# FFN output product in another order, one weight sum gathered early in loose slots, half-width rest rows, and sums of input weights begun elsewhere

## The chip, the cores and the metric

The kernel runs on one core of a Trainium2 chip. The metric is the device time of one execution in microseconds (us); a smaller number is better.

## What is computed

Two layers of a streaming encoder with 512 positions and 1024 channels. Each layer has a token mixer (three attention-like branches) and then an FFN. The change lies in the FFN alone:

```
u = einsum('bsd,df->bsf', x, w_ffn_in[l])          # 1024 -> 2 x 2816
u_gate, u_up = split(u, 2)
ffn = einsum('bsf,fd->bsd', silu(u_gate) * u_up, w_ffn_out[l])   # 2816 -> 1024
x = layer_norm(DEEPNORM_ALPHA * x + ffn, ln2_g[l], ln2_b[l])
```

## The kernel before

**Arithmetic.** Everything is float32. A matmul operand is split into a high and a low part in float32r, and a product is three matmuls (`mm3`, L125 to L127: high by high, and the two mixed ones). The high part is a cast on ScalarE (`wh`, L315 for a whole block, L157 for a Wt block), the low part a subtraction on VectorE (`wl`, L322, L158).

**Products by a two-by-two scheme.** A large product is cut into two by two blocks and made from seven products of sums of blocks in place of eight, in Winograd's form. The seven are called m1, m2, y, x, v, g and h. Each needs one weight block of 128 x 2048 elements (1 MB), which is a block of the weights or a sum of them, and each is 24 matmuls of 512 columns. Four of them add on to a bank that an earlier one left: x, then g, then h on m1's, and v on y's. VectorE reads such a bank between two of them (L1301 adds it to a row of the residual `z`; L852 and L857 do the same for the FFN's input). So v may not begin before VectorE has read y's banks.

**Where the sums come from.** A block is loaded by a DMA from the SP queue (`load`, L177) into a staging slot `st`, of which there are four. A second block is added to it in place by an accumulating DMA from the GpSimd queue (`more`, L181). In the class Chain, which FFN-out uses, one buffer serves m1, y, x and h in turn: when m1's block has been split, the next weights are accumulated onto it for y, then for x, then for h, so each of the accumulations waits for the split before it, and the next split for the accumulation. Its block c (for g) is a load and an accumulation in a staging slot of its own. In the class Close, which FFN-in uses, there are also a (for y) and c (for g), each a load and an accumulation.

**Order.** A list at the end of `layer` names the items in the order in which TensorE takes them. Each product is an item, with groups of small steps that are issued between its halves; `["c"]` and `["a"]` among them start a load and an accumulation. Blocks are split up to three items ahead (AHEAD = 3 buffers of `wh` and `wl`). Every engine and every queue works strictly in its own order: an instruction that waits holds all behind it.

**Names.** p, q, r and u are the four FFN-in groups (512 columns each, gate and up); t is the fifth one, whose 512 columns are not twinned into two-by-two products on the way out (its hidden blocks 16 to 19; blocks 20 and 21 come from `u_ffn`). o and w are the two FFN-out groups, of 8 hidden blocks each; `u_rest(0)` and `u_rest(1)` are the product of hidden blocks 16 to 21 with the remaining rows of w_ffn_out, for the left and the right half of the columns. Each u_rest has a block of four row tiles and a block of two. I write "w.y" for product y of group w, and so on. `s_hid` splits hidden blocks 16 to 21 for u_rest. `s_turn` transposes gate times up back with TensorE, in the middle of a product. Single tiles of 128 x 512 (activations, residual rows) come from another pool, `g`, with 61 slots.

Around the change the order before was: ... p.g, t.v, p.h, t.x, q.m1, t.g, q.y, t.h, q.v, q.m2, q.x, r.m1, q.g, r.y ..., and at the end of the layer ... u_rest(0), o.v, o.x, w.m1, o.g, w.m2, o.h, w.y, w.v, w.x, u_rest(1), w.g, w.h.

Of the kernel before, what the change touches and what calls it, by code (L numbers as in the profile page):

```python
# [17 lines left out]
P = 128  # L18
# [40 lines left out]
def trunk(ctx, tc, x_in, xT_in, w_in, ret_norm_g, da_norm_g, lq1, lk1, lq2, lk2, w_a, w_b, w_c, b_merge, w_out,  # L59
# [20 lines left out]
    def g(dt=F32, name="g"):  # L80
        return gp.tile([P, 512], dt, tag="g", name=name)
# [42 lines left out]
    def mm3(ps, lh, ll, rh, rl, start, stop, onto=False):  # L124
        nc.tensor.matmul(ps, lh, rh, start=start, stop=False, skip_group_check=onto)  # L125
        nc.tensor.matmul(ps, lh, rl, start=False, stop=False, skip_group_check=onto)  # L126
        nc.tensor.matmul(ps, ll, rh, start=False, stop=stop, skip_group_check=onto)  # L127
# [32 lines left out]
    class Halves:  # L160
# [30 lines left out]
        def g(self):  # L191
            return self.block(self.__dict__.pop("c"))

    class Chain(Halves):


# [34 lines left out]

        def h(self):
            return self.block(self.__dict__.pop("a"))

    class Close(Halves):

# [456 lines left out]
    def layer(l):  # L693
# [742 lines left out]
        def s_turn(pb, hf):  # L1436

            def fn():
                rows = [nat.pop((pb, 2 * hf + j)) for j in range(2)]
                for fp in range(2):  # L1440
                    ps = bank("ph")
                    for i in range(2):
                        for j in range(2):
                            o, c = 256 * i + P * j, P * (2 * fp + i)
                            nc.tensor.transpose(ps[:, o:o + P], rows[j][:, c:c + P], ident)
                    t = half[pb, hf, fp] = g(name="hf")
                    nc.scalar.copy(t, ps)
            return fn
# [11 lines left out]
        def s_differ(gi, fp):  # L1460
            def fn():
                twins[gi, fp].difference(half.pop((2 * gi + 1, 1, fp)))
            return fn

        def s_sums(gi, fp):
            def fn():
                twins[gi, fp].sums()
            return fn
# [6 lines left out]
        def s_hid(*ids):  # L1475
            def fn():
                for i in ids:
                    t, hid[i] = hid[i], Pair("hid")
                    split(hid[i], t)
            return fn  # L1480
# [13 lines left out]
        def s_natural(*ts):  # L1494
            def fn():
                for t in ts:
                    x1["n"].natural(t)
            return fn
# [20 lines left out]
        def fout_items(gi):  # L1519

            r0, kh = GROUPS[gi]
            hv = Chain(w_ffn_out[l], r0, kh)
            w = {}

            def it(name, *adds):
                def fn(wt):
                    if name == "m1" and gi == 0:
                        load_res(x2, saved[2 * l])
                        x2["n"] = Norm(x2["z"], v["g2"], v["b2"], None, None, xTs[l + 1],
                                       out if last else saved[2 * l + 1], xfs[l + 1])  # L1530
                    on = {"x": "m1", "g": "m1", "h": "m1", "v": "y"}.get(name, name)
                    final = gi == len(GROUPS) - 1 and name in ("m2", "g", "h")
                    for j in range(2):
                        end = last and final and name != "m2" and j
                        ps = w.pop((on, j), None)
                        for cols in (A, B) if end and name == "h" else (slice(0, 512),):
                            ps = product([hid[r0 + k] for k in range(kh)], name, j, wt, ps, cols)
                            for i, hf, op in adds:
                                plus(x2, 2 * i + j, hf, ps[:, cols], op, final, cols,
                                     (A, B) if end and name == "g" else (cols,))  # L1540
                        if name not in ("m2", "v", "h"):
                            w[on, j] = ps
                        if final and name == "h":
                            closed(2 + j)
                        between()
                    if final and name == "h" and not last:
                        quarters(l + 1)
                        ahead[nc.vector] = last_of(nc.vector)
                        behind[opening_fn[l + 1]] = list(ahead.values())
                return [getattr(hv, name)], fn  # L1550

            add, sub = ALU.add, ALU.subtract
            return {"c": hv.ahead_c, "m1": it("m1", (0, 0, add)), "y": it("y", (1, 1, add)), "x": it("x", (0, 1, sub)),
                    "m2": it("m2", (0, 0, add)), "v": it("v", (0, 1, add)), "g": it("g", (1, 1, sub)), "h": it("h", (1, 0, add))}

        ahead = {}
# [10 lines left out]
        def u_rest(hf):  # L1567

            rk = FT - REST - 4
            c0 = 512 * hf  # L1570
            blocks = [([w_ffn_out[l][P * REST:P * REST + P * 4, c0:c0 + 512]], 4),
                      ([w_ffn_out[l][P * REST + P * 4:P * FT, :]], rk)]

            def tile(t, b1, b2, midway=None):
                at = [(b1, k, 0) for k in range(4)] + [(b2, k, c0) for k in range(rk)]
                ps = bank("pf")
                for i, (w, k, c) in enumerate(at):
                    if i == len(at) // 2 and midway:
                        midway()
                    a, sl, cs = hid[REST + i], slice(P * t, P * t + P), slice(c, c + 512)  # L1580
                    mm3(ps, a.hi[:, sl], a.lo[:, sl], w.hi[:, k, cs], w.lo[:, k, cs], i == 0, i == len(at) - 1)
                plus(x2, t, hf, ps, ALU.add, hf and t < 2)
                if hf and t < 2:
                    closed(t)

            def fn(b1, b2):
                n = x2["n"]
                for t in range(NT):
                    tile(t, b1, b2, (lambda: n.transposes(0)) if hf and t == 3 and not last else None)
                    if hf and t == 0 and not last:  # L1590
                        opening[l + 1].early()
                    between()
            return blocks, fn

        def s_turn_rest(fp):
            def fn():
                for f in (fp, fp + 1):
                    ps = bank("ph")
                    for t in range(NT):
                        nc.tensor.transpose(ps[:, P * t:P * t + P], nat[4, t][:, P * f:P * f + P], ident)  # L1600
                    t = hid[REST + f] = g(name="fth")
                    nc.scalar.copy(t, ps)
            return fn
# [5 lines left out]
        for (specs, fn), *groups in [  # L1609
            (([ffn_opening.m1_high], p["m1"][1]), [], [s_turned(1)]), (([ffn_opening.m2_high], p["m2"][1]),),  # L1610
            (t["m1"], [], [s_x1(0)]), (t["m2"], [s_x1(1)], [s_x1(2)]), (u_ffn(20), [s_x1(3)], [s_x1r(0), p["c"]]),
            (p["y"], [s_x1r(1)], [s_x1r(2)]), (u_ffn(21), [s_x1r(3), t["a"]], [s_natural(0)]),
            (p["v"], [s_natural(1)]), (p["x"], [s_natural(2)]), (t["y"], [s_natural(3)]), (p["g"],), (t["v"], [s_turn(0, 0)]), (p["h"], [t["c"]], [q["a"]]),
            (t["x"], [s_turn(0, 1)]), (q["m1"],), (t["g"],), (q["y"],), (t["h"], [q["c"]]),
            (q["v"], [r["a"]]), (q["m2"], [s_turn_rest(0)]), (q["x"], [s_turn_rest(2)]), (r["m1"],), (q["g"],), (r["y"], [s_turn(1, 0)]), (q["h"], [r["c"]]),
            (r["v"], [u["a"]]), (r["m2"], [s_turn(1, 1)]), (r["x"],), (u["m1"],), (r["g"],), (u["y"], [s_turn(2, 0)]),
            (r["h"], [u["c"]], [s_ready(0, 0)]), (u["v"],), (u["m2"], [s_turn(2, 1)], [s_ready(0, 1)]), (u["x"],),
            (o["m1"], [s_differ(0, 0)], [s_differ(0, 1)]), (u["g"],), (o["m2"], [s_sums(0, 0)], [o["c"]]), (u["h"], [s_turn(3, 0), s_hid(16, 17)], [s_hid(18, 19)]),
            (o["y"], [s_sums(0, 1)], [s_hid(20, 21)]), (u_rest(0), [s_rest(0, 0)], [s_turn(3, 1)], [s_rest(0, 1)], [s_ready(1, 0)]), (o["v"],),
            (o["x"], [s_ready(1, 1)]),  # L1620
            (w["m1"], [s_differ(1, 0)]), (o["g"], [s_differ(1, 1)], [w["c"]]), (w["m2"], [s_sums(1, 0)]), (o["h"], [s_sums(1, 1)]),
            (w["y"], [s_rest(1, 0)]), (w["v"], [s_rest(1, 1)], [s_shift]), (w["x"],), (u_rest(1),),
            (w["g"], tail), (w["h"],),
        ]:
            item(specs, fn, *groups)
# [60 lines left out]
```

## Time and profile before

| what | value |
|---|---|
| median of three timed runs | 1890.74 us (1888.88 to 1890.86) |
| the profiled execution: its time, its span | 1887.43 us, 1885.7 us |
| TensorE busy | 1851.4 us, 98% of the span |
| VectorE busy, ScalarE busy | 1384.3 us (73%), 1024.9 us (54%) |
| mean granted TensorE clock | 0.993 |
| read from HBM, written | 289.79 MB, 22.07 MB |

The times of a trace count from the start of the span. TensorE's matmuls are pipelined, so one that is listed with 0.39 us follows its predecessor after 0.23 us. A row of a timeline gives the start, the duration, the engine, the line, the operation and the tiles (written <- read); in brackets is the idle time of that engine before it and what ended it. A "DMA" row in the chain of waits gives the time from the issue to the landing. The windows view gives for a stretch its length, and then for each engine its busy time, and last the granted TensorE clock (1.00 is full speed), the share of time in which the 16 DMA engines were busy, and GB/s.

### The profile page before, as it was taken

How to read it: one execution, taken by the hardware profiler on the slowest of the kernel's cores; microseconds unless marked ns; L12 is line 12 of the kernel's file. 1: busy time of each engine (PE TensorE's matmuls, PEld its weight loads, DVE VectorE, ACT ScalarE, POOL GpSimd, SP SyncE). 2: the span in 40 equal slices, each digit the busy share in tenths (PEclk: the TensorE clock that was granted, in tenths of full speed). 3: DMA queues.
4: the chain of work that ended last, by engine and by line, in shares of the span. 5: the costliest groups of instructions: out<-in, count | busy, mean ns of one | idle time of the engine just before them, and what ended most of it. 6: DMA issues, size and time to landing. Idle time of an engine off the chain costs nothing.

```text
span 1885.7 us, 23407 instructions
## 1 busy us (share of the span) xinstructions
PE 1851.4 (98%) x8766; PEld 1543.7 (82%) x8766; DVE 1384.3 (73%) x2100; ACT 1024.9 (54%) x1643; POOL 140.7 (7%) x156
## 2 busy tenths in 40 slices
PE   9999999999999999999999999999999999999988
PEld 8888888888888878877788888888888888788776
DVE  6876756777589866688696767567775998657986
ACT  5555654667547445564364556556674474445541
POOL 2001000000001000001020010000000010100010
PEclk9999999999999999999999999999999999999999
DMA  9684453332556877687585844532415667866782
GB/s 282 189 267 138 129 167 117 91 112 68 145 177 163 207 205 185 179 245 190 145 253 180 240 112 145 180 94 85 134 57 154 175 168 204 210 188 165 232 203 65
DMA packets 227809, 313.39 MB, mean 166 GB/s; under 512 B 8804, under 2 KB 111312, under 8 KB 227696
## 3 DMA queue, kind: packets, MB, share of 16 engines
q1 hardware_dynamic: 196128, 250.38, 40.4%
q0 software_dynamic: 31424, 61.26, 18.6%
q8 instruction: 69, 1.13, 0.3%
q14 instruction: 44, 0.36, 0.1%
q10 hardware_dynamic: 144, 0.26, 0.0%
HBM read 289.79 MB, written 22.07 MB: 165 GB/s over the span
## 4 chain that ended last, share of the span: by engine, by line
PE 85%; DMA 6%; DVE 5%; ACT 2%; issue 2%; POOL 0%; DVEq 0%; ACTq 0%; POOLq 0%; SPq 0%
PE pt L125 13%; PE pt L127 13%; PE pt L126 13%; PE pf L125 12%; PE pf L127 12%; PE pf L126 12%; DMA st<-in_w_ffn_in 4%; DVE wl L322 2%; DMA st<-in_w_ffn_out 2%; ACT wh L315 2%; PE ptr L503 1%; PE psc L464 1%; PE pco L1073 1%; PE psc L463 1%; PE pdo L1150 1%
## 5 line engine op out<-in xcount | busy, mean ns | idle before, releaser
L322 DVE TENSOR_TENSOR wl<-st,wh 128x2048 fp32r<-128x2048 f32 (+1 forms) x159 | 352.8, 2221 | 143.0 <-ACT wh L315 142.1
L315 ACT CAST wh<-st 128x2048 fp32r<-128x2048 f32 x154 | 294.3, 1913 | 249.4 <-PE pf L127 136.8
L125 PE MATMUL pt<-xTh,wh 128*128 128x512 f32 x832 | 327.6, 394 | 0.0
L127 PE MATMUL pt<-xTh,wl 128*128 128x512 f32 x832 | 324.5, 390 | 0.0
L126 PE MATMUL pt<-xTl,wh 128*128 128x512 f32 x832 | 324.3, 390 | 0.0
L158 DVE TENSOR_TENSOR wl<-st,wh 128x1024 fp32r<-128x1024 f32 (+2 forms) x174 | 185.5, 1085 | 61.2 <-ACT wh L157 48.0
L157 ACT CAST wh<-st 128x1024 fp32r<-128x1024 f32 (+2 forms) x174 | 159.7, 941 | 107.9 <-PE pt L126 60.8
L127 PEld LDWEIGHTS pt<-xTh,wl 128*128 128x128 f32 x832 | 156.3, 188 | 33.1
L125 PEld LDWEIGHTS pt<-xTh,wh 128*128 128x128 f32 x832 | 156.7, 188 | 31.0
L126 PEld LDWEIGHTS pt<-xTl,wh 128*128 128x128 f32 x832 | 156.5, 188 | 31.1
L125 PE MATMUL pf<-wh,xTh 128*128 128x512 f32 x384 | 151.3, 395 | 0.2
L126 PE MATMUL pf<-wl,xTh 128*128 128x512 f32 x384 | 149.5, 390 | 1.7 <-DVE wl L322 1.7
L127 PE MATMUL pf<-wh,xTl 128*128 128x512 f32 x384 | 149.5, 391 | 0.0
L125 PE MATMUL pf<-wh,s43h 128*128 128x512 f32 x288 | 114.5, 398 | 5.5 <-DVE tc L852 5.5
L125 PE MATMUL pf<-wh,s12h 128*128 128x512 f32 x288 | 113.8, 395 | 0.0
L126 PE MATMUL pf<-wl,s43h 128*128 128x512 f32 x288 | 113.5, 394 | 0.0
L127 PE MATMUL pf<-wh,s43l 128*128 128x512 f32 x288 | 113.1, 394 | 0.0
L126 PE MATMUL pf<-wl,s12h 128*128 128x512 f32 x288 | 112.4, 390 | 0.0
L127 PE MATMUL pf<-wh,s12l 128*128 128x512 f32 x288 | 111.8, 390 | 0.0
L842 ACT COPY tc<-pf 128x512 f32<-128x512 f32 x96 | 55.2, 588 | 83.1 <-PE pf L127 82.5
L125 PEld LDWEIGHTS pf<-wh,xTh 128*128 128x128 f32 x384 | 72.1, 188 | 16.9 <-ACT xTh L109 1.5
L126 PEld LDWEIGHTS pf<-wl,xTh 128*128 128x128 f32 x384 | 72.2, 188 | 16.8 <-DVE wl L322 2.5
(365 smaller groups left out, 3739.0 us busy)
## 6 DMA issues: line engine op xcount, KB each, us to landing
st<-in_w_in SPq DMA_DIRECT2D x53, 1024.0 KB, 5.8
st<-in_w_ffn_in SPq DMA_DIRECT2D x50, 1024.0 KB, 5.5
st<-in_w_in SPq DMA_DIRECT2D x48, 512.0 KB, 4.8
st<-in_w_ffn_in POOLq DMA_DIRECT2D x24, 1024.0 KB, 10.9
st<-in_w_ffn_out SPq DMA_DIRECT2D x24, 1024.0 KB, 8.0
st<-in_w_ffn_out POOLq DMA_DIRECT2D x16, 1024.0 KB, 10.1
st<-in_w_in POOLq DMA_DIRECT2D x12, 1024.0 KB, 11.5
th<-th SPq DMA_DIRECT2D x40, 256.0 KB, 4.1
```

The lines of the kernel that those rows point to most:

```text
L125: nc.tensor.matmul(ps, lh, rh, start=start, stop=False, skip_group_check=onto)
L126: nc.tensor.matmul(ps, lh, rl, start=False, stop=False, skip_group_check=onto)
L127: nc.tensor.matmul(ps, ll, rh, start=False, stop=stop, skip_group_check=onto)
L157: return [nc.scalar.copy(self.hi[:, a:b], self.st[:, a:b]), nc.vector.tensor_sub(self.lo[:, a:b], self.st[:, a:b], f(self.hi[:, a:b]))]
L158: nc.vector.tensor_sub(self.lo[:, a:b], self.st[:, a:b], f(self.hi[:, a:b]))]
L315: nc.scalar.copy(self.hi, st)
L322: nc.vector.tensor_sub(self.lo[:, k], self.st[:, k], f(self.hi[:, k]))
L463: yield nc.tensor.matmul(ps[:, :w], self.q[j][:, n], self.k[j][:, :w], start=True, stop=False)
L464: yield nc.tensor.matmul(ps[:, :w], self.q[j][:, n], self.kl[j][:, :w], start=False, stop=True)
L503: nc.tensor.transpose(ps[:, o + P * (nt - mt):o + P * (nt - mt) + P], E[pk][:, c + P * mt:c + P * mt + P], ident)
L842: nc.scalar.copy(t[to, j], ps)
L1073: pin(nc.tensor.matmul(*ops[k], start=k == order[0], stop=k == order[-1]))
```

## The change

It has five parts. The line numbers of the changed kernel are higher by 28 to 36 from the inserted classes on.

1. In group w the order becomes w.m1, o.g, w.m2, w.y, o.h, w.v, w.x: w.y and o.h are exchanged.
2. w's block c no longer uses a staging slot. Four tiles of 128 x 512 from the pool g take it (class Loose): four loads of 256 KB and four accumulations of 256 KB. They are issued in u_rest(0), four items earlier than before, and split by four small casts and subtractions just ahead of w.g.
3. u_rest loads only the half of the columns that it uses for its block of two row tiles (512 KB in place of 1 MB), and splits only that.
4. Sums of FFN-in begin elsewhere: t's c in p.g (before: p.h), q's a in the first half of p.h, r's a in q.m2 (before: q.v), u's a in r.m2 (before: r.v).
5. `s_hid` is issued one item earlier.

```
+    class Loose:
+        def __init__(self, hv, i, j):
+            self.hv, self.j, self.kh = hv, j, hv.kh
+            self.t = [g(name="wc") for _ in range(hv.kh)]
+            for k, t in enumerate(self.t):
+                nc.sync.dma_start(t, hv.src(i, j)[:, k])
+        def more(self, i):
+            for k, t in enumerate(self.t):
+                nc.gpsimd.dma_start(t, self.hv.src(i, self.j)[:, k], accum_op=ALU.add)
+        def block(self):
...
+            for k, t in enumerate(self.t):
+                split(Part(hi[:, k], lo[:, k]), t)
...
-                      ([w_ffn_out[l][P * REST + P * 4:P * FT, :]], rk)]
+                      ([w_ffn_out[l][P * REST + P * 4:P * FT, c0:c0 + 512]], rk)]
...
-            (w["m1"], [s_differ(1, 0)]), (o["g"], [s_differ(1, 1)], [w["c"]]), (w["m2"], [s_sums(1, 0)]), (o["h"], [s_sums(1, 1)]),
-            (w["y"], [s_rest(1, 0)]), (w["v"], [s_rest(1, 1)], [s_shift]), (w["x"],), (u_rest(1),),
+            (w["m1"], [s_differ(1, 0)]), (o["g"], [s_differ(1, 1)]), (w["m2"], [s_sums(1, 0)]), (w["y"], [s_sums(1, 1)]),
+            (o["h"], [s_rest(1, 0)]), (w["v"], [s_rest(1, 1)], [s_shift]), (w["x"],), (u_rest(1),),
```

Part 1 on VectorE, at the end of layer 0's FFN. In the rows before, wl_7614 is w.v's low part and wl_7654 is w.x's; z_7032 and z_7034 with pf_7658 and pf_7681 are the two reads of w.y's banks.

```order
L322 TENSOR_TENSOR wl_7614<-st_7611,wh_7613 128x2048
L1301 TENSOR_TENSOR z_7031<-z_7031,pf_7047 128x512
L1301 TENSOR_TENSOR z_7033<-z_7033,pf_7067 128x512
L115 TENSOR_TENSOR qgl_7726<-hf_6963,qgh_7725 128x512
L322 TENSOR_TENSOR wl_7654<-st_7416,wh_7653 128x2048
L1301 TENSOR_TENSOR z_7032<-z_7032,pf_7658 128x512
L115 TENSOR_TENSOR qhl_7730<-hf_7352,qhh_7729 128x512
L1301 TENSOR_TENSOR z_7034<-z_7034,pf_7681 128x512
```

In the changed kernel wl_7623 is w.v's low part, wl_7665 is w.x's, and pf_7626 and pf_7650 are w.y's banks.

```order
L358 TENSOR_TENSOR wl_7623<-st_7620,wh_7622 128x2048
L1337 TENSOR_TENSOR z_7032<-z_7032,pf_7626 128x512
L1337 TENSOR_TENSOR z_7034<-z_7034,pf_7650 128x512
L115 TENSOR_TENSOR qhl_7688<-hf_7357,qhh_7687 128x512
L358 TENSOR_TENSOR wl_7665<-st_7428,wh_7664 128x2048
```

The reads of w.y's banks stood behind the low part of w.x's block, and now stand ahead of it.

Part 4 on the SP queue, in the middle of layer 0's FFN-in. Before, st_6052 is the load for t.x, st_6097 q.m1's, st_6118 t's c and st_6136 q's a.

```order
L177 DMA st_6052<-in_w_ffn_in 128x4x512
L597 DMA saved0_80<-z_4814 128x512
L597 DMA saved0_80<-z_4815 128x512
L177 DMA st_6097<-in_w_ffn_in 128x4x512
L177 DMA st_6118<-in_w_ffn_in 128x4x512
L597 DMA saved0_80<-z_4816 128x512
L597 DMA saved0_80<-z_4817 128x512
L177 DMA st_6136<-in_w_ffn_in 128x4x512
```

Now st_6035 is t's c, st_6055 the load for t.x, st_6100 q.m1's and st_6121 q's a.

```order
L177 DMA st_6035<-in_w_ffn_in 128x4x512
L633 DMA saved0_80<-z_4814 128x512
L633 DMA saved0_80<-z_4815 128x512
L177 DMA st_6055<-in_w_ffn_in 128x4x512
L177 DMA st_6100<-in_w_ffn_in 128x4x512
L633 DMA saved0_80<-z_4816 128x512
L633 DMA saved0_80<-z_4817 128x512
L177 DMA st_6121<-in_w_ffn_in 128x4x512
```

t's c takes the first of these four places, and the loads for t.x and q.m1 move one place back each; q's a keeps its place.

Part 2 on the GpSimd queue, at the end of layer 0's FFN (st_6928 is o's chain and st_7428 w's, wc are the loose tiles).

```order
L181 DMA st_6928<-in_w_ffn_out 128x4x512
L205 DMA wc_7320<-in_w_ffn_out 128x512
L205 DMA wc_7321<-in_w_ffn_out 128x512
L205 DMA wc_7322<-in_w_ffn_out 128x512
L205 DMA wc_7323<-in_w_ffn_out 128x512
L181 DMA st_6928<-in_w_ffn_out 128x4x512
L181 DMA st_7428<-in_w_ffn_out 128x4x512 x3
```

Before, the accumulation for c stood between the first and the second of the three on w's chain; now its four pieces stand ahead of the last one on o's chain and all three on w's. On SP the four loads stand behind w.m2's load and ahead of w.v's.

More of the change, by code (lines that the diff above doesn't have):

```diff
@@ L192, in g, with __init__ @@
             return self.block(self.__dict__.pop("c"))
+    class Loose:
[8 more added lines that the diff above has]
+        def block(self):
+            self.nk = n = self.kh
+            hi, lo = (wsp.tile([P, 2048], F32R, tag=x, name=x)[:, :512 * n].rearrange("p (k c) -> p k c", k=n)
+                      for x in ("wh", "wl"))
+            self.hi, self.lo = hi, lo
+            for k, t in enumerate(self.t):
+                split(Part(hi[:, k], lo[:, k]), t)
+            return self
+    class Part:
+        def __init__(self, hi, lo):
+            self.hi, self.lo = hi, lo
     class Chain(Halves):
@@ L233, in h, with loose_c, g @@
             return self.block(self.__dict__.pop("a"))
+        def loose_c(self):
+            self.c = Loose(self, 0, 1)
+            self.c.more(1)
+        def g(self):
+            c = self.__dict__.pop("c")
+            return c.block() if isinstance(c, Loose) else self.block(c)
     class Close(Halves):
@@ L1552, in fout_items @@
             add, sub = ALU.add, ALU.subtract
-            return {"c": hv.ahead_c, "m1": it("m1", (0, 0, add)), "y": it("y", (1, 1, add)), "x": it("x", (0, 1, sub)),
+            return {"c": hv.loose_c if gi else hv.ahead_c, "m1": it("m1", (0, 0, add)), "y": it("y", (1, 1, add)), "x": it("x", (0, 1, sub)),
                     "m2": it("m2", (0, 0, add)), "v": it("v", (0, 1, add)), "g": it("g", (1, 1, sub)), "h": it("h", (1, 0, add))}
@@ L1571, in u_rest @@
             blocks = [([w_ffn_out[l][P * REST:P * REST + P * 4, c0:c0 + 512]], 4),
-                      ([w_ffn_out[l][P * REST + P * 4:P * FT, :]], rk)]
+                      ([w_ffn_out[l][P * REST + P * 4:P * FT, c0:c0 + 512]], rk)]
             def tile(t, b1, b2, midway=None):
-                at = [(b1, k, 0) for k in range(4)] + [(b2, k, c0) for k in range(rk)]
+                at = [(b1, k) for k in range(4)] + [(b2, k) for k in range(rk)]
                 ps = bank("pf")
-                for i, (w, k, c) in enumerate(at):
+                for i, (w, k) in enumerate(at):
                     if i == len(at) // 2 and midway:
                         midway()
-                    a, sl, cs = hid[REST + i], slice(P * t, P * t + P), slice(c, c + 512)
-                    mm3(ps, a.hi[:, sl], a.lo[:, sl], w.hi[:, k, cs], w.lo[:, k, cs], i == 0, i == len(at) - 1)
+                    a, sl = hid[REST + i], slice(P * t, P * t + P)
+                    mm3(ps, a.hi[:, sl], a.lo[:, sl], w.hi[:, k], w.lo[:, k], i == 0, i == len(at) - 1)
                 plus(x2, t, hf, ps, ALU.add, hf and t < 2)
@@ L1612, in layer @@
             (p["y"], [s_x1r(1)], [s_x1r(2)]), (u_ffn(21), [s_x1r(3), t["a"]], [s_natural(0)]),
-            (p["v"], [s_natural(1)]), (p["x"], [s_natural(2)]), (t["y"], [s_natural(3)]), (p["g"],), (t["v"], [s_turn(0, 0)]), (p["h"], [t["c"]], [q["a"]]),
+            (p["v"], [s_natural(1)]), (p["x"], [s_natural(2)]), (t["y"], [s_natural(3)]), (p["g"], [t["c"]]), (t["v"], [s_turn(0, 0)]), (p["h"], [q["a"]]),
             (t["x"], [s_turn(0, 1)]), (q["m1"],), (t["g"],), (q["y"],), (t["h"], [q["c"]]),
-            (q["v"], [r["a"]]), (q["m2"], [s_turn_rest(0)]), (q["x"], [s_turn_rest(2)]), (r["m1"],), (q["g"],), (r["y"], [s_turn(1, 0)]), (q["h"], [r["c"]]),
-            (r["v"], [u["a"]]), (r["m2"], [s_turn(1, 1)]), (r["x"],), (u["m1"],), (r["g"],), (u["y"], [s_turn(2, 0)]),
+            (q["v"],), (q["m2"], [s_turn_rest(0)], [r["a"]]), (q["x"], [s_turn_rest(2)]), (r["m1"],), (q["g"],), (r["y"], [s_turn(1, 0)]), (q["h"], [r["c"]]),
+            (r["v"],), (r["m2"], [u["a"]], [s_turn(1, 1)]), (r["x"],), (u["m1"],), (r["g"],), (u["y"], [s_turn(2, 0)]),
             (r["h"], [u["c"]], [s_ready(0, 0)]), (u["v"],), (u["m2"], [s_turn(2, 1)], [s_ready(0, 1)]), (u["x"],),
-            (o["m1"], [s_differ(0, 0)], [s_differ(0, 1)]), (u["g"],), (o["m2"], [s_sums(0, 0)], [o["c"]]), (u["h"], [s_turn(3, 0), s_hid(16, 17)], [s_hid(18, 19)]),
-            (o["y"], [s_sums(0, 1)], [s_hid(20, 21)]), (u_rest(0), [s_rest(0, 0)], [s_turn(3, 1)], [s_rest(0, 1)], [s_ready(1, 0)]), (o["v"],),
+            (o["m1"], [s_differ(0, 0)], [s_differ(0, 1)]), (u["g"], [s_hid(16, 17)], [s_hid(18, 19)]), (o["m2"], [s_sums(0, 0)], [o["c"]]), (u["h"], [s_turn(3, 0)], [s_hid(20, 21)]),
+            (o["y"], [s_sums(0, 1)]), (u_rest(0), [s_rest(0, 0), w["c"]], [s_turn(3, 1)], [s_rest(0, 1)], [s_ready(1, 0)]), (o["v"],),
             (o["x"], [s_ready(1, 1)]),
-            (w["m1"], [s_differ(1, 0)]), (o["g"], [s_differ(1, 1)], [w["c"]]), (w["m2"], [s_sums(1, 0)]), (o["h"], [s_sums(1, 1)]),
-            (w["y"], [s_rest(1, 0)]), (w["v"], [s_rest(1, 1)], [s_shift]), (w["x"],), (u_rest(1),),
+            (w["m1"], [s_differ(1, 0)]), (o["g"], [s_differ(1, 1)]), (w["m2"], [s_sums(1, 0)]), (w["y"], [s_sums(1, 1)]),
+            (o["h"], [s_rest(1, 0)]), (w["v"], [s_rest(1, 1)], [s_shift]), (w["x"],), (u_rest(1),),
             (w["g"], tail), (w["h"],),
```

## The prediction

> **What bounds the kernel now.** TensorE is busy for 98% of the span and no matmul is added or taken away, so the change can win only what TensorE waits, with the half clock that follows a long wait. I read TensorE's waits first.
>
> ```profile
> PE pf L125 <- DVE z L1301: 13.3, 3, 6.4
> PE pf L125 <- DVE tc L852: 5.5, 2, 3.1
> PE pf L127 <- DVE hidl L115: 3.2, 4, 1.7
> PE pf L126 <- DVE wl L322: 1.7, 2, 1.2
> ```
>
> These are sums over both layers, all in the FFN. I call them the end stall (z), the stall at t.g (tc), that at u_rest(0) (hidl) and that at r.m1 (wl). The two long kinds are also followed by a slow clock. The windows view, with the wait and the stretch behind it, for layer 0 (t.g, then the end) and layer 1 (the same):
>
> ```profile
> 685.97:689.07 3.10, 0.00 (x0) 0.03 (x1) 3.00 (x3) 0.99 (x3) 0.00 (x0) 1.00 0.99 181
> 689.07:693.07 4.00, 4.00 (x11) 3.17 (x12) 2.70 (x4) 2.77 (x4) 0.00 (x0) 0.57 0.85 265
> 893.15:899.58 6.43, 0.00 (x1) 0.03 (x1) 3.04 (x3) 4.31 (x4) 0.00 (x0) 0.87 0.61 236
> 899.58:905.08 5.50, 5.50 (x14) 4.35 (x15) 3.43 (x5) 0.00 (x0) 1.28 (x1) 0.54 0.66 98
> ```
>
> ```profile
> 1624.36:1626.80 2.44, 0.00 (x1) 0.03 (x1) 2.41 (x3) 0.34 (x1) 0.00 (x0) 1.00 1.13 207
> 1626.80:1632.80 6.00, 6.00 (x19) 4.79 (x20) 4.40 (x5) 4.68 (x4) 0.00 (x0) 0.72 0.62 182
> 1829.49:1835.89 6.40, 0.00 (x0) 0.03 (x1) 3.03 (x3) 4.31 (x4) 0.45 (x1) 0.78 0.63 244
> 1835.89:1840.89 5.00, 5.00 (x14) 3.96 (x15) 3.41 (x5) 0.00 (x0) 0.83 (x1) 0.60 0.73 115
> ```
>
> A stretch at clock c loses its length times (1 - c). The end stall costs 6.43 + 0.46 x 5.50 = 8.96 in layer 0 and 6.40 + 0.40 x 5.00 = 8.40 in layer 1, together 17.4 us. The stall at t.g costs 3.10 + 0.43 x 4.00 = 4.82 and 2.44 + 0.28 x 6.00 = 4.12, together 8.9 us. With 3.2 and 1.7 all four are worth 31.2 us.
>
> **The end stall.** The chain of waits there:
>
> ```profile
> 865.50 0.23 PE pf L126
> ...
> 876.60 0.24 PE pf L127
> ...
> 878.86 2.30 DVE wl L322
> ...
> 881.44 13.07 DMA st<-in_w_ffn_out
> ...
> 894.61 1.91 ACT wh L315
> ```
>
> w.y's split ends at 881.2, the accumulation for w.x takes 13.07, w.x's cast comes at 894.61. VectorE sits in front of w.x's low part, and the reads of w.y's banks, which w.v needs, stand behind that. Two things end this. The order puts the reads of w.y ahead of w.x's low part, and w.y is split one product earlier relative to w.x's use. From 865.50 to 876.60 are 49 matmuls, 0.2265 each, so a product of 24 takes 5.44.
>
> Without a stall before it, w.y then starts where o.h did, at 893.15 - 2 x 5.44 = 882.3, and w.x three products later, at 898.6. w.y's sum is the accumulation issued at 861.48, and its twin in layer 1 at 1797.8:
>
> ```profile
> L181 POOL DMA_DIRECT2D st<-in_w_ffn_out x1: 1282/1282/1282, 861.5 to 861.5; - x1
> DMA to landing us min/median/max: 13.7/13.7/13.7
> ```
>
> ```profile
> L181 POOL DMA_DIRECT2D st<-in_w_ffn_out x1: 1282/1282/1282, 1797.8 to 1797.8; - x1
> DMA to landing us min/median/max: 14.9/14.9/14.9
> ```
>
> It lands at 875.2; cast 1.9 and low part 2.3 make w.y ready at 879.5, 2.8 ahead of 882.3. In layer 1 it lands at 1812.7, ready at 1817.0 against 1829.49 - 10.88 = 1818.6: 1.6 to spare. The next accumulation starts near 879.8. Even at 13.07 it lands at 892.9 and w.x is ready at 897.1, 1.5 ahead; and the 1 MB accumulation for c and 512 KB of u_rest's load have left its company, so I expect less. I take the full 17.4 us. What hides w.y now is only these 2.8 and 1.6 us.
>
> **w's c in loose tiles.** Four loads and four accumulations of 256 KB go out behind w.m2's load, while the DMA engines idle:
>
> ```profile
> 849.00:859.00 10.00, 10.00 (x46) 8.27 (x45) 9.62 (x14) 4.87 (x4) 0.00 (x0) 1.00 0.01 2
> ```
>
> They are wanted when w.x ends, near 904. Their low parts are four of the small kind in place of one of 2.29:
>
> ```profile
> L158 DVE TENSOR_TENSOR wl<-st,wh 128x512 fp32r<-128x512 f32 x38 | 25.4, 687 | 14.7 <-PE ptr L503 8.6 <-ACT wh L157 5.8
> ```
>
> 4 x 0.69 = 2.8, half a microsecond more, under u_rest(1) of 72 matmuls (16.3 us). Zero on the path. Queued behind the four on GpSimd are o's last and w's first accumulation, which before went out at 861.5; only if the loose loads landed after that would it cost.
>
> **u_rest and s_hid.** The half load and half split take away work, and hidden blocks are split ahead of u_rest(0). Two of the six low parts still stand behind a read of o.y's bank, but u_rest(0) uses them 12 matmuls (2.7 us) after its start. I take the whole 3.2.
>
> **Sums of FFN-in.** r.m1 waited for its own load, issued late and slowed by two accumulations:
>
> ```profile
> 697.35 4.95 DMA st<-in_w_ffn_in
> ...
> 712.20 10.32 DMA st<-in_w_ffn_in
> ```
>
> Now r.m1's load goes in the place of r's a, and r's a in that of r.m1. I take the 1.7. r's a is then loaded at 712 less what is gained; a load of 5 (the first of these rows), an accumulation of 11 and a split of 4.2 make 732 to 733, against r.y's start, five products and its transposes later, at about 735; covered, but by 2 us. u's a moves in the same way.
>
> t's c is the hard one. Now:
>
> ```profile
> 663.05 5.94 DMA st<-in_w_ffn_in
> ...
> 669.85 14.16 DMA st<-in_w_ffn_in
> ...
> 684.09 1.92 ACT wh L315
> ...
> 686.03 2.29 DVE wl L322
> 688.32 0.61 DVE tc L852
> ```
>
> The loads, on SP's queue:
>
> ```profile
> 651.01 0.38 SPq L177 DMA_DIRECT2D st<-in_w_ffn_in  x1
> ...
> 660.25 3.19 SPq L177 DMA_DIRECT2D st<-in_w_ffn_in  x2
> ...
> 670.50 42.07 SPq L177 DMA_DIRECT2D st<-in_w_ffn_in  x6
> ```
>
> The load in the first place goes out at 651.01, so t's c is accumulated from about 656.7 and lands by 671 even at 14.16. t.g's split is then done near 680 and the wait of 3.10 goes. But this accumulation now runs beside the load for t.x, which is issued at 660. What does that load take? Alone it would take 4.95, like the load at 697.35; beside an accumulation the nearest rows are these (a load issued 1.2 us behind one):
>
> ```profile
> st<-in_w_ffn_in POOLq DMA_DIRECT2D x1, 1024.0 KB, 11.0
> st<-in_w_ffn_in SPq DMA_DIRECT2D x1, 1024.0 KB, 10.4
> ```
>
> and, for the load issued at 673.5 beside two, this:
>
> ```profile
> DMA to landing us min/median/max: 13.6/13.6/13.6
> ```
>
> I take 10.4: it lands at 670.6. VectorE's addition on to it (which now starts at 668.1) frees the slot for q's a:
>
> ```profile
> L283 DVE TENSOR_TENSOR st<-st x1: 2285/2285/2285, 668.1 to 668.1; 128x2048 f32<-128x2048 f32 x1
> ```
>
> So q's a is loaded at 672.9 in place of 670.50. Load 5.1 and accumulation 0.6 + 11.0 (the row with one load beside it) land it at 689.6; cast and low part make q.y ready at 693.8. TensorE, without the stall at t.g, wants q.y at 685.97 + 5.44 = 691.4. So 2.4 us are lost again, at q.y or at t.x's transposes, which need a VectorE result that stands behind q.m1's late low part:
>
> ```profile
> 674.83 0.69 DVE L1433 TENSOR_TENSOR fth<-tc,fth 128x512 f32<-128x512 f32 x1 [0.75 <-ACT fth L1425]
> ```
>
> ```profile
> 676.73 1.04 PE L1445 MATMUL ph<-ident,fth 128*128 128x128 f32 x8
> ```
>
> There only 1.2 us are to spare. Split over both places the waits are too short for the slow clock (the rows with 1.2 and 1.7 us of waiting show none behind them). With 5.0 for the load, q's a is as early as before and nothing is lost: the gain is 8.9. With 13.6, q.y is ready 3.2 + 1.3 later still: about 7 us wait and 1.7 of clock per layer, 8.5 or so lost in all against before. I take 8.9 - 2 x 2.4 = 4.1.
>
> The Trainium skill, "DMA: Bandwidth & Descriptors", section "Queues, rings and completion order", says that each DMA engine takes turns between the queue rows it has work for. By that the load for t.x would get half and land within about 9 us, which would leave some 1 us lost and a sum 2 to 3 us better; the row of 10.4 agrees no more than roughly, and I keep it.
>
> **The sum.** 17.4 + 3.2 + 1.7 + 4.1 = 26.4 us. From the profiled execution's 1887.43 that is 1861.0; it lay 3.3 under the median of the timed runs, and from the median of 1890.74 it is 1864.3, my forecast.
>
> **The rivals.** (a) Everything goes, as the load for t.x isn't slowed: 31.2 us, 1859.5. For it: DMA engines are little used before 660. (b) The stall at t.g only moves to q.y, as long as it was or longer: 26.4 - 4.1 = 22.3 us and down to 14, 1868.4 to 1877. For it: the rows of 13.6 and 14.16. The Trainium skill, "TensorE: Matmul & The Clock Gate", section "What's actually happening", puts the halved clock behind an idle window of some 3.4 us; the rows here show it behind 2.44 already. By the rule (b) would keep 3.4 us of clock, by the rows it wouldn't. (c) w.y becomes the late block, since it has one product less: an accumulation 5 us longer than 13.7 and 14.9 leaves waits of 2.2 and 3.4 us with their clock, about 9 us: 1873. Against it: the company of that accumulation doesn't grow. (d) Slower: GpSimd's queue is held by the four loose accumulations (their tiles or loads late), and w's first accumulation behind them starts X late. w.y then waits X - 2.2 and about 2.3 of clock in each layer; the gain of 13.2 per layer is used up, and 1.9 beyond it, at X = 15, when the last loose load lands after 876. At X = 20 it is 1904. Against it: the loads go out right behind w.m2's load, the second of two issued from 842.30:
>
> ```profile
> 842.30 22.89 SPq L177 DMA_DIRECT2D st<-in_w_ffn_out  x2
> ```
>
> The Trainium skill, "DMA: Bandwidth & Descriptors", section "Anatomy of one DMA — SWDGE (gpsimd) path", counts about 2 us of fixed time per DMA, which for eight in place of two would be an estimated 12 us more in series; that is still inside the time up to 859. (e) The moves do nothing: other waits of equal length follow, 1889.
>
> **How the numbers follow.** Forecast 0.52, (a) 0.17, (b) 0.18, (c) 0.07, (d) 0.03, (e) 0.03. The range goes from the profiled time less everything, 1856, to most of (b) and (c), 1875. Faster by over 0.2% (3.8 us, about what a measurement can tell here) are the first four, 0.94; within it 0.03, slower 0.03.
>
> **What would show it.** In the profile after, no wait of TensorE for z at w.v, and w.x's cast no later than the end of o.h; the waits for hidl and at r.m1 gone; short waits at t.x's transposes or q.y, in sum 2 to 3 us per layer; the load for t.x landing near 670. A wait at w.y, or loose accumulations after 859, would make it wrong.

## The result and the profile after

| | median us | ratio to the kernel before, 95% interval | profiled execution: time, span |
|---|---|---|---|
| before | 1889.81 (1888.27 to 1890.86, 4 runs) | | 1887.43, 1885.7 |
| changed | 1859.97 (1858.54 to 1862.54, 4 runs) | 0.9844 (0.9827 to 0.9861) | 1859.39, 1857.6 |

The change gains 29.8 us of the medians and 28.0 between the two profiled executions. The forecast was 26.4 and 1864.3. All readings below are of undisturbed executions; the profile of one experiment (e4) was disturbed and isn't read.

The waits of TensorE in the changed kernel (in total, times, longest):

```profile
PE pf L126 <- DVE wl L358: 2.1, 2, 1.4
PE pf L125 <- DVE z L1337: 1.3, 2, 0.8
PE ph L1481 <- DVE fth L1469: 1.0, 2, 0.7
PE pf L127 <- DVE hidl L115: 0.2, 1, 0.2
```

The 13.3 for z is down to 1.3 (0.5 of it at the end of the program, as before, and 0.8 new at u_rest(0) in layer 1). The 5.5 for tc and the waits at r.m1 are gone, and 3.2 for hidl is 0.2. What is new is what the prediction placed at t.x's transposes (fth) and q.y (wl). The windows: first the wait at q.y in layer 0 and the stretch behind it, then w.y, o.h and w.v at the end of that layer.

```profile
691.73:693.14 1.41, 0.01 (x1) 0.01 (x1) 1.35 (x1) 1.41 (x1) 0.00 (x0) 1.00 0.00 0
693.14:698.14 5.00, 5.00 (x22) 4.15 (x23) 4.58 (x4) 2.79 (x3) 0.00 (x0) 1.00 0.23 32
```

```profile
874.70:890.00 15.30, 15.30 (x70) 12.65 (x69) 15.30 (x18) 7.39 (x7) 1.28 (x1) 1.00 0.89 238
```

No slow clock follows the short wait, and TensorE is busy for all of the 15.30 us that hold the former stall. There, in the changed kernel, w.y's low part, w.y's first matmul and w.x's cast:

```profile
868.43 2.29 DVE L358 TENSOR_TENSOR wl<-st,wh 128x2048 fp32r<-128x2048 f32 x1 [2.44 <-ACT wh L351]
```

```profile
874.77 0.39 PE L125 MATMUL pf<-wh,qyh 128*128 128x512 f32 x1
```

```profile
880.41 1.92 ACT L351 CAST wh<-st 128x2048 fp32r<-128x2048 f32 x1 [2.96 <-PE pf L127]
```

w.y is ready at 870.7 and used at 874.8: 4.1 us to spare, where 2.8 was forecast. In layer 1 it is ready at 1796.2 and used at 1798.9, with 2.6 to spare where 1.6 was forecast. ScalarE's wait before w.x's cast was ended by TensorE, which freed a buffer, and no longer by a DMA. The accumulation for w.x took 8.7 in place of 13.07:

```profile
st<-in_w_ffn_out POOLq DMA_DIRECT2D x1, 1024.0 KB, 8.7
```

The chain of waits that leads to the new wait at q.y in layer 0, with the load of q.m1's block first, the accumulation of q's a second; and the load for t.x in layer 0, from the list of DMA issues:

```profile
662.79 8.50 DMA st<-in_w_ffn_in
...
677.20 11.55 DMA st<-in_w_ffn_in
...
688.85 1.92 ACT wh L351
...
690.79 2.30 DVE wl L358
```

```profile
st<-in_w_ffn_in SPq DMA_DIRECT2D x1, 1024.0 KB, 8.6
```

q's a lands at 688.75 and q.y's split ends at 693.1; the forecast had 689.6 and 693.8. The load for t.x takes 8.6 in layer 0 and 9.6 in layer 1.

### The profile page after: what moved, and what is told of

It reads as the page before. It is cut to its first block, busy times and chain, and to the rows that moved or that the text cites. A ratio compares the mean times of both kernels' runs of the same rounds, so it can differ in the third digit from the quotient of the medians.

```text
span 1857.6 us, 23450 instructions
## 1 busy us (share of the span) xinstructions
PE 1841.9 (99%) x8766; PEld 1538.2 (83%) x8766; DVE 1379.6 (74%) x2106; ACT 1020.5 (55%) x1649; POOL 145.3 (8%) x162
## 4 chain that ended last, share of the span: by engine, by line
PE 91%; DVE 4%; DMA 3%; ACT 1%; issue 1%; SPq 0%; DVEq 0%; POOL 0%; ACTq 0%; POOLq 0%
PE pf L125 14%; PE pf L127 14%; PE pf L126 14%; PE pt L125 13%; PE pt L127 13%; PE pt L126 13%; DMA st<-in_w_ffn_in 2%; DVE wl L358 1%; PE ptr L539 1%; PE psc L500 1%; PE pco L1109 1%; PE psc L499 1%; ACT wh L351 1%; PE pdo L1186 1%; PE ph L1481 1%
## 5 line engine op out<-in xcount | busy, mean ns | idle before, releaser
L358 DVE TENSOR_TENSOR wl<-st,wh 128x2048 fp32r<-128x2048 f32 (+1 forms) x157 | 348.4, 2221 | 145.0 <-ACT wh L351 143.7
L351 ACT CAST wh<-st 128x2048 fp32r<-128x2048 f32 x152 | 290.2, 1913 | 246.2 <-PE pf L127 117.6
L158 DVE TENSOR_TENSOR wl<-st,wh 128x1024 fp32r<-128x1024 f32 (+2 forms) x174 | 181.4, 1061 | 58.3 <-ACT wh L157 45.3
L125 PEld LDWEIGHTS pt<-xTh,wh 128*128 128x128 f32 x832 | 156.3, 188 | 31.2 <-ACT xTh L706 0.3
L127 PEld LDWEIGHTS pf<-wh,xTl 128*128 128x128 f32 x384 | 72.1, 188 | 16.0 <-DVE xTl L115 0.6
```

What stands on the lines that cost most here:

```text
L158: nc.vector.tensor_sub(self.lo[:, a:b], self.st[:, a:b], f(self.hi[:, a:b]))]
L351: nc.scalar.copy(self.hi, st)
L358: nc.vector.tensor_sub(self.lo[:, k], self.st[:, k], f(self.hi[:, k]))
```

## The experiments

The theory: each part ends its own stall, worth 17.4 (end), 8.9 less what comes back at q.y (t.g), 3.2 (hidl) and 1.7 (r.m1). The rivals: a stall only moves to the next late block, or a part does nothing beside another. Six kernels are the kernel before with one part alone, four the changed kernel with one part undone, and two change what is left at q.y. The half-width block and the order were not undone in the changed kernel.

| kernel | median us | ratio to before, 95% interval | span of the profile |
|---|---|---|---|
| e1: order of w.y and o.h alone | 1870.06 | 0.9894 (0.9878 to 0.9910) | 1868.2 |
| e2: loose tiles alone | 1875.36 | 0.9923 (0.9908 to 0.9938) | 1876.1 |
| e3: t's c, q's a alone | 1892.09 | 1.0009 (0.9996 to 1.0021) | 1890.9 |
| e4: r's a, u's a alone | 1887.35 | 0.9983 (0.9971 to 0.9994) | not read |
| e5: half-width block alone | 1886.38 | 0.9989 (0.9980 to 0.9999) | 1884.8 |
| e6: s_hid alone | 1891.34 | 1.0016 (1.0007 to 1.0025) | 1888.5 |
| n1: changed, without t's c, q's a | 1865.51 | 0.9867 (0.9852 to 0.9881) | 1863.2 |
| n2: changed, without r's a, u's a | 1870.70 | 0.9894 (0.9879 to 0.9909) | 1865.8 |
| n3: changed, without s_hid | 1863.71 | 0.9854 (0.9837 to 0.9870) | 1863.2 |
| n4: changed, without loose tiles | 1860.19 | 0.9840 (0.9825 to 0.9855) | 1860.8 |
| e7: changed, t.x's load before t's c | 1860.69 | 0.9855 (0.9841 to 0.9869) | 1861.9 |
| e8: changed, t.h's block on t.x's slot | 1856.03 | 0.9830 (0.9817 to 0.9843) | 1855.8 |

n1 to n4 shared a chip, and so did e7 and e8.

**e1, the order alone.**

```
-(w["m2"], [s_sums(1, 0)]), (o["h"], [s_sums(1, 1)]), (w["y"], [s_rest(1, 0)]), (w["v"], ...
+(w["m2"], [s_sums(1, 0)]), (w["y"], [s_sums(1, 1)]), (o["h"], [s_rest(1, 0)]), (w["v"], ...
```

> The kernel before with w.y and o.h exchanged and nothing else; w's c stays in a staging slot, its accumulation still second on w's chain. Theory (the order ends the end stall): no wait for z at w.v in either layer, 6.43 and 6.40 us of waiting and the slow clock behind them gone, 17.4 us, so 1889.8 - 17.4 = 1872.4, or up to 3 us more if c's accumulation makes w.x's late (a wait of up to 1.5 us per layer at w.x). Rival (c's accumulation in the company of w's is what made the stall, and the order only moves it): a wait of 3 to 6 us per layer appears at w.y or w.x, and the time is 1880 or more.

Its waits, and the accumulation for w.x:

```profile
PE pf L125 <- DVE tc L852: 5.7, 2, 3.3
...
PE pf L125 <- DVE z L1301: 0.5, 1, 0.5
```

```profile
st<-in_w_ffn_out POOLq DMA_DIRECT2D x1, 1024.0 KB, 12.0
```

Both waits at w.v are gone and the span is 17.5 shorter (the ratio gives 17.0 to 23.1): the whole of the forecast 17.4, with c's accumulation still there and w.x's still at 12.0. The order alone ends the stall.

**e2, the loose tiles alone.** Class Loose, and `w["c"]` in u_rest(0) in place of o.g; the old order.

> The kernel before with w's c in loose tiles, gathered in u_rest(0), and the old order of w.y and o.h. Theory: the accumulation for w.x is alone and takes 9 to 9.5 us in place of 13.07, w.x's cast and w.v's bank reads come some 3.5 us earlier, a wait of about 3 us per layer stays at w.v with a shorter slow clock; 8 to 10 us gained, 1880 to 1882. Rival (c's company is the whole cause): no wait at w.v, 1872. Second rival (c was hidden anyway): the wait stays 6.4, 1890.

```profile
PE pf L125 <- DVE z L1337: 5.1, 3, 2.9
```

```profile
st<-in_w_ffn_out POOLq DMA_DIRECT2D x1, 1024.0 KB, 8.3
```

Alone on the queues the accumulation takes 8.3. Waits of 1.7 and 2.9 stay at w.v, and the span is 9.6 shorter (the ratio gives 11.7 to 17.4). The loose tiles remove over half of the stall by shortening the transfer that the order makes harmless: the two parts work on the same 17.4.

**n4, the changed kernel without the loose tiles.**

```
-return {"c": hv.loose_c if gi else hv.ahead_c, ...
+return {"c": hv.ahead_c, ...
```

> The changed kernel with w's c in a staging slot again, begun in o.g. Theory (the order alone ends the end stall, and the loose tiles add nothing to that): no wait at w.v, w.x's accumulation takes 12 us in place of 8.7 and still lands in time; 1860 to 1862. Rival (with the earlier stalls gone TensorE reaches the end sooner, and the two accumulations beside each other are late again): a wait of 2 us or more per layer at w.x, w.v or w.g, 1865 or more.

```profile
PE pf L126 <- DVE wl L358: 4.2, 3, 1.8
```

```profile
st<-in_w_ffn_out POOLq DMA_DIRECT2D x1, 1024.0 KB, 12.9
```

```profile
1817.50:1818.60 1.10, 0.00 (x2) 0.01 (x1) 1.10 (x2) 1.10 (x3) 0.00 (x0) 1.00 0.53 203
```

One wait of 1.10 at w.x in layer 1 is all that the rival gets. The time is that of the changed kernel: what e2 gained alone is worth nothing measurable beside the new order.

**e3, t's c and q's a alone.**

```
-(p["g"],), (t["v"], ...), (p["h"], [t["c"]], [q["a"]]),
+(p["g"], [t["c"]]), (t["v"], ...), (p["h"], [q["a"]]),
```

> The kernel before with t's c begun in p.g and q's a in the first half of p.h, and nothing else. Theory: both waits at t.g go with their slow clock (8.9 us), and some 1.6 us per layer come back at t.x's transposes and at q.y, as in the changed kernel; 5.7 us gained, 1884. Rival (the wait only moves to q.y): a wait of 3 us or more there with the half clock behind it, 1888 to 1890.

```profile
PE pf L125 <- DVE z L1301: 14.8, 3, 7.4
PE pf L126 <- DVE wl L322: 7.0, 5, 1.8
PE pf L127 <- DVE hidl L115: 3.5, 4, 1.8
```

```profile
694.20:699.20 5.00, 5.00 (x15) 3.97 (x16) 4.60 (x4) 2.76 (x3) 0.00 (x0) 0.66 0.21 43
...
1664.90:1669.00 4.10, 4.10 (x11) 3.29 (x12) 4.07 (x4) 3.15 (x4) 0.00 (x0) 0.60 0.72 241
```

My theory fell here. The waits for tc are gone, but those for wl rose from 1.7 to 7.0: at q.y in both layers, and again at r.m1. A slow clock follows q.y in layer 0 (0.66) and r.m1 in layer 1 (0.60), and also the wait for hidl in layer 1, now 1.8 us long (0.66 from 1776.62 to 1781.60). The end stall is 1.5 us longer. Nothing is gained.

**e4, r's a and u's a alone.** `r["a"]` from q.v to q.m2 and `u["a"]` from r.v to r.m2.

> The kernel before with r's a begun in q.m2 and u's a in r.m2, and nothing else. Theory: the waits at r.m1 (1.24 and 0.45 us) go and none comes at r.y or u.y; 1.7 us gained, 1888, within what a measurement tells. Rival: r's a, now loaded last, makes r.y late by 1 to 3 us, and the time is 1890 to 1894.

1.1 to 5.5 us are gained; 1.7 lies in that. That the waits at r.m1 went in this kernel is not shown.

**n1, the changed kernel without the move of t's c and q's a** (e3's edit undone).

> The changed kernel with t's c and q's a begun where they were before. Moving them gained nothing when it was the only edit. Theory (it does gain where r.m1 and the end don't give it back): the waits at t.g, 3.1 and 2.4 us with their slow clock, are back, those at t.x's transposes and q.y (1.55 and 1.62 us) go; 5.7 us slower than the changed kernel, 1865 to 1866. Rival (the move is worth nothing anywhere): 1859 to 1861.

```profile
PE pf L125 <- DVE tc L888: 5.9, 2, 3.4
```

As the theory said: 5.5 us slower by the medians and 5.6 in span, the waits for tc are back, those at q.y gone. The intervals of the two ratios overlap, but all runs of n1 (1864.01 to 1866.08) lie above all of n4 on the same chip (1857.85 to 1862.65). The same move is worth nothing alone and some 5 us in this kernel.

**n2, the changed kernel without the move of r's a and u's a** (e4's edit undone).

> The changed kernel with r's a and u's a begun where they were before. Theory: as with t's c moved alone, r.m1 waits 1.7 us per layer and q.y some 1 us more, and a slow clock follows where a wait is over 2 us; 4 to 6 us slower than the changed kernel, 1864 to 1866. Rival (they are worth only the 1.7 us seen before): 1861 to 1862.

```profile
PE pf L126 <- DVE wl L358: 6.0, 4, 1.8
PE pf L125 <- ACT wh L351: 1.6, 2, 1.4
```

The load of r.m1's block in layer 0, the two waits behind it, and the stretch that follows:

```profile
708.87 12.14 DMA st<-in_w_ffn_in
```

```profile
723.04 0.50 PE L125 MATMUL pf<-wh,xTh 128*128 128x512 f32 x1 [1.38 <-ACT wh L351]
725.36 0.79 PE L126 MATMUL pf<-wl,xTh 128*128 128x512 f32 x1 [1.82 <-DVE wl L358]
```

```profile
725.36:730.00 4.64, 4.64 (x14) 3.69 (x15) 4.50 (x5) 3.55 (x5) 0.00 (x0) 0.66 0.79 255
```

It is slower than n4, on the same chip, by 10.5 us, and in span by 8.2 than the changed kernel, more than either reading. r.m1 waits for its cast and its low part in both layers. The reason is e3's. r.m1's load goes out 3.3 us earlier than in the kernel before, but takes 12.1 in place of 10.3 and lands only 1.5 earlier, at 721.0. TensorE, with the stall at t.g gone, is there 4 us earlier (721.66 in place of 725.65). A wait that was 1.2 us long behind another stall is 3.2 without it, and a slow clock follows. The two moves belong together: n1 and n2 show what each is worth beside the other, e3 and e4 that alone it is little or nothing. No run undoes both; an estimate of their worth together is n1's 5.5 and e4's 1.1 to 5.5, so 6.6 to 11.0 us.

**e5, the half-width block alone.**

```
-([w_ffn_out[l][P * REST + P * 4:P * FT, :]], rk)]
+([w_ffn_out[l][P * REST + P * 4:P * FT, c0:c0 + 512]], rk)]
...
```

> The kernel before with the half-width block in u_rest alone. Theory: the split of the block of two row tiles, 1.1 us shorter on VectorE, stands ahead of the hidden blocks' low parts, so the waits for hidl at u_rest(0) (1.89 and 1.29 us) shrink by about 1.1 each; about 2 us gained, 1888. Rival (s_hid's place is the whole cause): waits unchanged, 1890.

```profile
PE pf L127 <- DVE hidl L115: 2.2, 6, 0.7
```

3.2 is down to 2.2, and 0.2 to 3.8 us are gained.

**e6, s_hid alone.** `s_hid` for blocks 16 to 19 from u.h to u.g, for 20 and 21 from o.y to u.h.

> The kernel before with s_hid one item earlier alone. Theory: the hidden blocks' low parts stand earlier on VectorE, the waits for hidl go but for some tenths; about 3 us gained, 1887. Rival (the bank read in front of them holds them as before): waits unchanged, 1890.

```profile
PE pf L125 <- DVE z L1301: 17.6, 5, 8.0
...
PE pf L127 <- DVE hidl L115: 0.4, 2, 0.2
```

```profile
892.10:900.20 8.10, 0.06 (x2) 0.07 (x1) 3.08 (x3) 4.31 (x4) 0.03 (x1) 0.67 0.54 203
900.20:905.20 5.00, 5.00 (x12) 3.95 (x13) 3.28 (x4) 0.00 (x0) 1.25 (x1) 0.51 0.64 105
```

Neither reading held: the waits for hidl go as said, and the kernel is slower by 1.3 to 4.7 us. The end stall takes over what was saved (8.04 in place of 6.43 in layer 0, 7.67 in place of 6.40 in layer 1), and 0.3 and 1.1 of the 17.6 are new waits for banks at u_rest(0). TensorE comes 1.0 us earlier, and the accumulation that sets the end stall also goes out 1.0 earlier (881.44 in the kernel before), but it takes 14.65 in place of 13.07 and lands 0.6 later. Why it took longer stays open.

```profile
880.44 14.65 DMA st<-in_w_ffn_out
```

**n3, the changed kernel without s_hid's move.**

> The changed kernel with s_hid one item later, as before. The earlier place made the kernel before slower by 3 us when it was the only edit. Theory (what it gained was handed to the end stall, which is gone now): waits for hidl of 2 to 3 us in sum are back; 2 to 3 us slower than the changed kernel, 1862 to 1863. Rival (the earlier place costs by itself, as it holds back bank reads): 1857 to 1859, faster than the changed kernel.

```profile
PE pf L126 <- DVE wl L358: 3.3, 2, 1.8
...
PE pf L127 <- DVE hidl L115: 2.2, 7, 0.5
```

The waits for hidl are back, 2.0 us more than in the changed kernel, and the 0.8 for z at u_rest(0) is gone. The median is 3.7 higher, but the intervals overlap, and the waits at the transposes and at q.y, which this edit doesn't touch, are 1.9 longer in sum, with a slow clock behind one. The rival isn't met: no run of n3 is faster than 1861.16. The worth of s_hid's place in this kernel is 1 to 2 us by the waits; the times don't show it.

**e7, t.x's load first.**

```
-(p["g"], [t["c"]]), (t["v"], [s_turn(0, 0)]),
+(p["g"],), (t["v"], [t["c"], s_turn(0, 0)]),
```

> The changed kernel with the load for t.x ahead of t's c (t's c in t.v in place of p.g). Theory (what is left at q.y is set by VectorE's order: the addition that frees q's a its slot stands behind t.x's low part): the load for t.x takes 5.1 us alone, but the addition comes only 0.6 us earlier, t's c is accumulated beside q's a, q.y waits as long as before or 1 us longer; 1860 to 1862. Rival (the load that shares with an accumulation, 8.6 us in place of 5.1, is the cause): the waits at t.x's transposes and q.y go, 3.2 us gained, 1857.

The load for t.x, and on VectorE the low part of t.x and the addition that frees q's a its slot; then the same addition in the changed kernel:

```profile
st<-in_w_ffn_in SPq DMA_DIRECT2D x1, 1024.0 KB, 5.0
```

```profile
665.54 2.29 DVE L358 TENSOR_TENSOR wl<-st,wh 128x2048 fp32r<-128x2048 f32 x1
667.74 2.29 DVE L319 TENSOR_TENSOR st<-st 128x2048 f32<-128x2048 f32 x1
```

```profile
668.62 2.29 DVE L319 TENSOR_TENSOR st<-st 128x2048 f32<-128x2048 f32 x1 [0.66 <-DMA st<-in_w_ffn_in]
```

The load goes out 9.4 us earlier and takes 5.0 in place of 8.6, but the addition stands behind t.x's low part and starts only 0.9 earlier. q.y waits as long as before or longer (1.82 against 1.41 in layer 0): t's c is now accumulated beside the load of q's a, which takes 7.7 in place of 5.7. So the slow load for t.x cost the addition little: in the changed kernel it waited 0.66 for that load, and 1.68 in layer 1. The rest is the slot, which is free only behind t.x's low part and the addition.

**e8, one slot less.** t.h's block is accumulated on to t.x's slot behind its split.

```
+class Onto(Early):
+    def x(self):
+        b = self.block(self.d)
+        self.more(self.d, 1, 0)
+        return b
+    def h(self):
+        return self.block(self.__dict__.pop("d"))
-... u_fin(4, Early), ...
+... u_fin(4, Onto), ...
```

> The changed kernel, with t.h's block accumulated onto t.x's slot once that is split, in place of a load and an addition on VectorE. It takes one slot less, so q's a is loaded some 8 us earlier, at about 663. Theory (the slot is what makes q's a late): its accumulation lands by 684, the waits at t.x's transposes and q.y go, 3 us gained and 2 x 2.3 us of VectorE, 1857. Rival (three accumulations within 15 us slow each other and the loads): q.m1's load or t's c lands late, the wait moves there, 1860 to 1864.

This also puts one accumulation in place of a load and an addition of 2.29 us on VectorE in each layer. The load of q's a on SP, its cast, and the waits of TensorE:

```profile
662.26 0.38 SPq L177 DMA_DIRECT2D st<-in_w_ffn_in  x1
```

```profile
681.61 1.91 ACT L362 CAST wh<-st 128x2048 fp32r<-128x2048 f32 x1 [3.96 <-DMA st<-in_w_ffn_in]
```

```profile
PE pf L127 <- DVE hidl L115: 1.6, 3, 1.1
...
PE pf L125 <- DVE tc L904: 1.2, 1, 1.2
...
PE pf L126 <- DVE wl L369: 0.3, 1, 0.3
```

q's a is loaded 8.7 us earlier, its sum is cast at 681.6 in place of 688.9, and the waits at the transposes and q.y go. In their place 1.2 us of waiting for tc appear in layer 1. How much of the gain is the slot's and how much the addition's, no run separates. Its five runs (1855.34 to 1857.56) lie below all of e7 (1859.20 to 1863.66) on the same chip. It is the fastest kernel of the study, about 4 us ahead of the changed one by the medians; the intervals of the two ratios still overlap.

## Why the prediction was right

- **The end stall, 17.4.** Right in place and size (e1: 17.5). Of the two reasons given, order and less company for the accumulation, the first is enough; the second would have given over half alone (e2) and adds nothing measurable (n4). Costing loose tiles at nothing on the path was right.
- **t.g, 8.9 less 4.8.** The waits at t.g went and part came back at the transposes and at q.y, as forecast. TensorE idled 1.55 and 1.62 us there in this execution where 2.4 per layer was forecast. With the same instructions there, n2 shows 1.5 and 1.6, and e3, n3 and n4 show 1.8 to 3.0 per layer, in one layer of each with a slow clock, so 2.4 lies inside what the runs show. One step of its reasoning isn't borne out: "With 5.0 for the load, q's a is as early as before and nothing is lost". e7 has that load at 5.0 and q's a as early as before (670.09 against 670.50), and loses 1.8 and 2.6; but t's c then slows the load of q's a, so e7 is not the case that the sentence meant. The load for t.x took 8.6 and 9.6, not 10.4. The rule cited from the Trainium skill, "DMA: Bandwidth & Descriptors", section "Queues, rings and completion order", gave an estimate of about 9, which was nearer than the row that I took; its sum, 2 to 3 us better than mine, was 28.4 to 29.4, against 28.0 measured.
- **r.m1, 1.7.** Right as the wait that the profile showed (it is gone in the changed kernel, and e4's gain covers it), but mis-sized as a term of this sum: n2 loses 8 to 10 us, as the repair of t.g would have turned it into 3.2 and 2.1 us with a slow clock. That the sum came out was luck in this term: the change made both moves.
- **hidl, 3.2.** 3.0 of the waits went and 0.8 came back at a bank of u_rest(0), so the term came out 1.0 short. That a stall ahead of a longer one is worth its length was taken without a reason; in the kernel before it was worth less than nothing (e6).
- **The sum.** What is left of the four stalls is 4.2 us (1.55, 1.62, 0.8 and 0.2), so 27.0 of 31.2 went by the rows: 1.6 more than forecast at t.g and 1.0 less at hidl. The other 1.0 of the 28.0 no row shows, and runs of one kernel differ by 4 us. Of the rivals, (a) has the time (1859.5) and not the mechanism, since the load for t.x was slowed and its stalls did not all go; (b) is what e3 shows for t's c alone; (c) and (d) didn't come: w.y had 4.1 and 2.6 us to spare, and the accumulation behind the loose ones waited for a split and not for them.

## What to carry to other kernels

The worth of a stall is what is left of it once the others are gone: a transfer that doesn't come earlier by as much as TensorE does makes a longer wait, so add up waits only for edits that are made together, and look at the next late block behind each. Two edits on one stall were worth the larger one here, not the sum; exchanging two products did alone what a second staging path did in part. Where a sum is late, look for what frees its slot before you blame the speed of its load.

## What the runs showed of the hardware

**A wait well under 3 us can halve the clock, and the same wait may not.** n4 (first three rows) and e7 (last two), the wait at q.y in layer 0 and the stretch behind it:

```profile
691.49:693.32 1.83, 0.00 (x1) 0.01 (x1) 1.77 (x1) 1.83 (x2) 0.00 (x0) 1.00 0.00 0
693.83:697.24 3.41, 3.41 (x9) 2.64 (x9) 3.41 (x4) 1.67 (x1) 0.00 (x0) 0.50 0.05 7
697.24:702.00 4.76, 4.76 (x22) 3.90 (x22) 4.48 (x2) 2.11 (x3) 0.41 (x1) 1.00 0.62 216
```

```profile
691.35:693.17 1.82, 0.00 (x1) 0.01 (x1) 1.76 (x1) 1.82 (x2) 0.00 (x0) 1.00 0.00 0
693.20:700.00 6.80, 6.80 (x30) 5.66 (x31) 6.39 (x5) 4.05 (x5) 0.00 (x0) 1.00 0.43 137
```

The slow stretch is 3.41 us long; behind the 8.04 us of waiting in e6 it is 10.24, three times that:

```profile
894.82:905.06 10.24, 4.90 (x12) 3.88 (x13) 6.36 (x6) 4.31 (x4) 1.28 (x1) 0.50 0.45 106
```

The Trainium skill, "TensorE: Matmul & The Clock Gate", section "What's actually happening", has a free-running window of 3413 ns; the lengths agree with that, and so does a wait of 1.8 us that counts once and not another time. That an idle window of some 3.4 us is needed first does not agree with n4's 1.83.

**A 1 MB load beside one accumulation** took 8.6 and 9.6 us in the two layers against 5.0 alone (the changed kernel and e7), and a 1 MB accumulation 8.3 alone against 12.0 to 14.65 beside another and loads (e2, e1, e6).
